# Token tiles kept in DRAM, gate stores issued by GpSimd, and MLP taps over both sequences at once, in a two-layer hybrid encoder

## The chip, the cores and the metric

The kernel runs on one core of a Trainium2 chip. Its engines are TensorE (PE, with its weight loads as PEld), VectorE (DVE), ScalarE (ACT), GpSimd (POOL) and SyncE (SP), whose instructions here only start transfers. The metric is the device time of one execution in microseconds, as the median of several runs; lower is better.

## The reference

Two sequences (a prompt of 512 tokens, a sample of 256) go through two layers of an encoder with shared weights, width 1024. What each layer computes, cut to what matters here:

```python
proj = rmsnorm(x, norm_mix) @ w_in            # z, xbc, dt, ret q/k/v/g, na q/k/v, gates
xbc  = silu(dwconv(xbc))                      # xs (512), B and C (2 x 128 each)
o_ssd = rmsnorm((bidir_scan(C, B, xs*dt_f, dt_f*a0, xs*dt_b, dt_b*a1) + d*xs) * silu(z))
o_ret = rmsnorm(bidir_scan(rotary(q), rotary(k), v)) * silu(g)      # retention
o_na  = neighborhood_attention(q, k, v, rpb)                         # on a grid 64 wide
gates = sigmoid(gates + gate_bias)
merged = sum(gates[:, :, i] * (o_i @ w_branch[i]) for i in range(3))
x = x + merged @ w_out
u = dwconv(rmsnorm(x) @ ffn_w_up)             # 3 taps a channel, zero beyond each sequence's ends
val, gt = split(u)                            # 2816 channels each
x = x + (silu(gt) * val) @ ffn_w_down
```

The scans are computed in chunks of 128 tokens: inside a chunk by a decayed score matrix, between chunks by states that run forwards and backwards.

## The kernel before

Both sequences lie side by side, T = 768 tokens in NT = 6 chunks of 128: chunks 0 to 3 are the prompt, 4 and 5 the sample. Every large product is made of three products of a high and a low part: a weight block arrives as wraw (L197, two buffers), ACT makes its high part whi (L206) and DVE the low part wlo (L207), six slots each; the products stand at L366 to L368, L388 to L390 (token-major jobs) and L492 to L494 (pairs of products).

The main stream of PE is this sequence of products: the input projection, then the gate products in pairs, then the branch products, the output projection and the MLP. The three mixers are generators (`ssd()`, `ret()`, `na()`), and `load_o()` is a fourth; a class `Side` takes a piece of one of them between main products. So their small products share PE with the main stream. The final order of each engine is set by a scheduler that simulates a timeline over the whole program; each engine then runs its instructions strictly in that order, waiting where an operand isn't there. All DMAs are issued by SP, in one row of 948 instructions, and each waits there for its operands and buffers.

The places that the change touches:

- **SSD tokens.** xbc lies in DRAM with channels in rows. `load(c)` (L762) brings a chunk as xt. `tokens(xt)` (L767) turns four blocks of it into xs (128 tokens x 512) and two into btok (128 x 256): six transposes on PE (L330, tiles xsT and bT) and two copies by ACT (L772, L777). `back(cs)` (L798) does that for chunks 3, 2, 1 and later for 5, to run the states backwards: `state()` weights xs by DVE (xw, L782) and multiplies on PE (st, L785). The chunk loop (L806) then does it again for all six chunks, since xs and btok have two buffers each. It makes the scores sc (L817), loads four decay rows a chunk, spread over partitions (cw, L827), which ACT shifts in four operations (L833) and DVE subtracts (L834), multiplies into po (L846), and on POOL starts y (L851).
- **Gates.** `gates()` (L1184): when the pair of products pg and pv is done, ACT takes its tanh (L1186) and SP stores each half to gate_scr (L1187, 384 KB each). Twelve pairs a layer; the last two take buffers of the pool that the branch loop uses. The branch loop (L1222) loads gate tiles back (g, L1233), multiplies on PE (L366 to L368) and gates the result on DVE (merged, L1238).
- **MLP.** `conv(s)` in `up()` (L1281) takes the three taps of a channel block: ACT the centre (L1285), DVE the two outer ones (L1287, L1289), once for the prompt's 512 columns and once for the sample's 256, then SiLU or the product. There are 88 of these in all.

Of the kernel before, what the change touches and what calls it, by code (L numbers as in the profile page):

```python
# [6 lines left out]
F32 = mybir.dt.float32  # L7
F32R = mybir.dt.float32r
I32 = mybir.dt.int32
AF = mybir.ActivationFunctionType  # L10
OP = mybir.AluOpType

P = 128
# [3 lines left out]
TP = 512  # L17
# [266 lines left out]
def body(tc, nc, a, depth=DEPTH):  # L284
# [303 lines left out]
    def layer(l, x_in, prev_x):  # L588
# [32 lines left out]
        nkl_scr = dram.tile([4, P, T], F32, name=f"nkl_scr{l}")  # L621
        gate_scr = dram.tile([24, P, T], F32, name=f"gate_scr{l}")
        cum_scr = dram.tile([4 * NT, 512], F32, name=f"cum_scr{l}")
        t1_scr = dram.tile([3, P, 512], F32, name=f"t1_scr{l}")
        o_scr = [dram.tile([T, 512], F32, name=f"o_scr{l}_{b}") for b in range(3)]

# [84 lines left out]
        def ssd():  # L711
# [55 lines left out]
            def tokens(xt):  # L767
# [9 lines left out]
                act(b, ps[:, :256], AF.Copy)  # L777
                return xs, b

            def state(xs, b, d, c, prev, tag, bufs):  # L780
                xw = nt([P, 8, 64], "xw", "rx", 1)
                tt(xw, xs.rearrange("p (h c) -> p h c", c=64), bc(ex[:, d, c, :, None], [P, 8, 64]), op=OP.mult)  # L782
                ps = mxbank("st", "mx")
                for g in range(2):
                    mm(ps[:, g * 256:(g + 1) * 256], b[:, g * P:(g + 1) * P],  # L785
                       xw[:, g * 4:g * 4 + 4, :], start=True, stop=True)
                new = nt([P, 512], "new", tag, bufs)
                if prev is None:
                    act(new, ps, AF.Copy)
                else:  # L790
                    tt(new.rearrange("p (h c) -> p h c", c=64), prev.rearrange("p (h c) -> p h c", c=64),
                       bc(ex[:, 4 + d, c, :, None], [P, 8, 64]), op=OP.mult)
                    tt(new, new, ps, op=OP.add)
                return new
# [3 lines left out]
            def back(cs):  # L798
                for c in cs:
                    xt = load(c)  # L800
                    xs, b = tokens(xt)
                    yield
                    pb[c - 1] = state(xs, b, 1, c, pb[c], "pb", 5)
                    yield

            for c in range(NT):  # L806
# [3 lines left out]
                xt = load(c)  # L810
                zt = nt([P, 512], "zt", "ld2", 1)
                nc.sync.dma_start(zt, z_scr[c * P:(c + 1) * P])
                xs, b = tokens(xt)
                x3 = xs.rearrange("p (h c) -> p h c", c=64)
                sc = mxbank("sc", "my")
                for g in range(2):
# [367 lines left out]
        def gates(i, pool, tag, bufs, pump):  # L1184
            def evac(j, g):
                act(g, g, AF.Tanh, bias=gbh[:, i + j:i + j + 1], scale=0.5)  # L1186
                nc.sync.dma_start(gate_scr[i + j], g)  # L1187

            pair(pool, tag, bufs, pump, evac)

# [84 lines left out]
        def up(i):  # L1275
# [5 lines left out]
            def conv(s):  # L1281
                r, u = raw[s], ftile("u", ("uv", "ug")[s])
                f = i + NFF * s
                w = lambda j: par[:, O_FW + f * 3 + j:O_FW + f * 3 + j + 1]
                act(u, r, AF.Identity, scale=w(1), bias=par[:, O_FB + f:O_FB + f + 1])  # L1285
                for c0, n in RANGES:
                    stt(u[:, c0 + 1:c0 + n], r[:, c0:c0 + n - 1], w(0), u[:, c0 + 1:c0 + n],  # L1287
                        op0=OP.mult, op1=OP.add)
                    stt(u[:, c0:c0 + n - 1], r[:, c0 + 1:c0 + n], w(2), u[:, c0:c0 + n - 1],  # L1289
                        op0=OP.mult, op1=OP.add)  # L1290
                us[s] = u
                if s == 1:
                    act(u, u, AF.Silu)
                    return
                ah, al = out
                tt(u, u, us[1], op=OP.mult)
                act(ah, u, AF.Copy)
                tt(al, u, ah.bitcast(F32), op=OP.subtract)
# [101 lines left out]
```

## Time and profile before

| | |
|---|---|
| median of 3 runs | 2604.86 us (2600.97 to 2606.41) |
| the profiled execution | 2605.65 us, its span 2603.9 us |
| mean granted clock of TensorE | 0.995 |
| busy: PE, DVE, ACT, POOL | 2560.1, 1904.2, 1153.4, 87.8 us |
| DMA | 359.65 MB, mean 138 GB/s |
| SSD in the trace | about 126 to 300 us in layer 0, 1416 to 1590 us in layer 1 |
| branch products begin | at about 622 us and 1915 us |
| MLP | up to 1290 us and up to 2584 us |

The span is the profiled execution from its first to its last instruction; the device time has a little around it. A row of a view names the line, the engine, the operation and the tiles as out<-in; in brackets stands how long the engine was idle before it, and what ended that.

### The profile page before, as it was taken

Reading aid. Unit: us, or ns where it says so; the run is one execution under the profiler, and the core shown is the slowest. Engines: PE = TensorE matmul, PEld = TensorE weight load, DVE = VectorE, ACT = ScalarE, POOL = GpSimd, SP = SyncE. Lnnn points to the kernel's source line nnn. Section 1 sums busy time; section 2 is a strip of 40 time slices with the busy share of each in tenths; the row PEclk is TensorE's granted clock in tenths of the full one; section 3 lists DMA queues with packets and bytes.
Section 4 is the critical chain, followed back from the end, with each engine's and each line's share of the span. In section 5 each row is a group of like instructions: output and inputs, shape, how many; then the busy total and the mean of one; then the engine's idle time right before and its main releaser. Section 6 shows DMA issues by size and latency. Waiting matters only on the chain.

```text
span 2603.9 us, 37538 instructions
## 1 busy us (share of the span) xinstructions
PE 2560.1 (98%) x14290; PEld 2353.6 (90%) x14290; DVE 1904.2 (73%) x3204; ACT 1153.4 (44%) x1946; POOL 87.8 (3%) x130
## 2 busy tenths in 40 slices
PE   8999999999999999999999999999999999999998
PEld 8878999999889999999998789999998899999997
DVE  6758876665658887888866688765657598888887
ACT  5434465553235433333454455655432354333343
POOL 0002100000000000000000011100000000000000
PEclk9999999999999999999999999999999999999999
DMA  7356568747522222222453575787474222212222
GB/s 248 108 169 204 190 213 255 223 134 230 158 81 67 67 70 73 65 68 71 135 174 129 163 233 172 219 236 215 132 230 141 73 89 65 62 60 73 74 66 89
DMA packets 168900, 359.65 MB, mean 138 GB/s; under 512 B 16080, under 2 KB 62480, under 8 KB 168720
## 3 DMA queue, kind: packets, MB, share of 16 engines
q1 hardware_dynamic: 168720, 357.25, 43.5%
q8 instruction: 113, 1.85, 0.3%
q14 instruction: 67, 0.55, 0.1%
HBM read 276.87 MB, written 80.31 MB: 137 GB/s over the span
## 4 chain that ended last, share of the span: by engine, by line
PE 85%; DMA 7%; ACT 3%; DVE 3%; issue 1%; SPq 1%; POOL 0%; DVEq 0%; POOLq 0%; ACTq 0%
PE acc L493 12%; PE acc L492 12%; PE acc L494 12%; PE dn L1344 5%; PE dn L1342 5%; PE dn L1343 5%; PE acc L366 4%; PE acc L368 4%; PE acc L367 4%; PE acc L389 3%; PE acc L388 3%; PE acc L390 3%; PE wo L390 2%; PE wo L388 2%; PE wo L389 2%
## 5 line engine op out<-in xcount | busy, mean ns | idle before, releaser
L206 ACT ACTIVATE whi<-wraw 128x1024 fp32r<-128x1024 f32 (+2 forms) x444 | 433.8, 985 | 616.0 <-DMA wraw<-wp 153.3
L207 DVE TENSOR_TENSOR wlo<-wraw,whi 128x1024 fp32r<-128x1024 f32 (+2 forms) x444 | 500.3, 1132 | 189.2 <-ACT whi L206 186.9
L493 PE MATMUL acc<-hTl,whi 128*128 128x384 f32 x1216 | 414.3, 341 | 5.0 <-DVE hTl L435 5.0
L492 PE MATMUL acc<-hTh,whi 128*128 128x384 f32 x1216 | 414.1, 341 | 2.9 <-ACT pt L498 2.0
L494 PE MATMUL acc<-hTh,wlo 128*128 128x384 f32 x1216 | 410.0, 339 | 0.0
L492 PE MATMUL acc<-Eh,whi 128*128 128x384 f32 x912 | 309.3, 340 | 0.9 <-DVE pv L498 0.9
L494 PE MATMUL acc<-Eh,wlo 128*128 128x384 f32 x912 | 307.4, 338 | 0.0
L493 PE MATMUL acc<-El,whi 128*128 128x384 f32 x912 | 306.9, 337 | 0.0
L493 PEld LDWEIGHTS acc<-hTl,whi 128*128 128x128 f32 x1216 | 230.3, 189 | 7.5 <-DVE hTl L435 6.0
L492 PEld LDWEIGHTS acc<-hTh,whi 128*128 128x128 f32 x1216 | 229.9, 189 | 7.4 <-ACT pt L498 3.5
L494 PEld LDWEIGHTS acc<-hTh,wlo 128*128 128x128 f32 x1216 | 229.9, 189 | 0.4
L389 PE MATMUL acc<-wlo,hTh 128*128 128x512 f32 (+1 forms) x576 | 210.1, 366 | 2.6 <-DVE wlo L207 2.6
L388 PE MATMUL acc<-whi,hTh 128*128 128x512 f32 (+1 forms) x576 | 208.8, 364 | 2.9 <-ACT whi L206 2.6
L390 PE MATMUL acc<-whi,hTl 128*128 128x512 f32 (+1 forms) x576 | 209.2, 365 | 0.0
L1343 PE MATMUL dn<-wlo,ah 128*128 128x512 f32 x528 | 207.4, 393 | 0.0
L1344 PE MATMUL dn<-whi,al 128*128 128x512 f32 x528 | 201.8, 394 | 0.0
L1342 PE MATMUL dn<-whi,ah 128*128 128x512 f32 x528 | 200.4, 393 | 0.0
L1357 DVE TENSOR_TENSOR x<-x,dn 128x512 f32<-128x512 f32 x168 | 111.9, 685 | 86.0 <-PE dn L1344 86.0
L366 PE MATMUL acc<-hTh,whi 128*128 128x256 f32 (+1 forms) x512 | 174.0, 340 | 0.0
L492 PEld LDWEIGHTS acc<-Eh,whi 128*128 128x128 f32 x912 | 171.3, 188 | 2.9 <-DVE pv L498 1.9
L368 PE MATMUL acc<-hTh,wlo 128*128 128x256 f32 (+1 forms) x512 | 172.9, 338 | 0.0
L367 PE MATMUL acc<-hTl,whi 128*128 128x256 f32 (+1 forms) x512 | 172.9, 338 | 0.0
(277 smaller groups left out, 4772.3 us busy)
## 6 DMA issues: line engine op xcount, KB each, us to landing
wraw<-wp SPq DMA_DIRECT2D x284, 512.0 KB
g<-gate_scr SPq DMA_DIRECT2D x48, 384.0 KB
cw<-cum_scr SPq DMA_DIRECT2D x48, 256.0 KB
xt<-xbc_scr SPq DMA_DIRECT2D x20, 512.0 KB
bias<-nab SPq DMA_DIRECT2D x40, 256.0 KB
gate_scr<-pg SPq DMA_DIRECT2D x24, 384.0 KB
gate_scr<-pv SPq DMA_DIRECT2D x24, 384.0 KB
ot<-o_scr SPq DMA_DIRECT2D x36, 256.0 KB
```

Source lines behind the costliest of these rows:

```text
L206: self.nc.scalar.activation(hi[:, :n], r, AF.Copy)
L207: self.nc.vector.tensor_tensor(lo[:, :n], r, hi[:, :n].bitcast(F32), op=OP.subtract)
L366: mm(o, wh[:, k, :], rh, start=(k == 0), stop=False)
L388: mm(o, hT[0][:, k, ts_], wh[:, cs], start=(k == 0), stop=False)
L389: mm(o, hT[0][:, k, ts_], wl[:, cs], start=False, stop=False)
L390: mm(o, hT[1][:, k, ts_], wh[:, cs], start=False, stop=(k == NK - 1))
L492: mm(o, w[0][:, k, :], r[0][:, k, :], start=first and k == 0, stop=False, skip_group_check=True)
L493: mm(o, w[0][:, k, :], r[1][:, k, :], start=False, stop=False, skip_group_check=True)
L494: mm(o, w[1][:, k, :], r[0][:, k, :], start=False, stop=k == 3, skip_group_check=True)
L1342: mm(ps, ah[:, tsl], wh[:, cs], start=(j == 0), stop=False)
L1343: mm(ps, ah[:, tsl], wl[:, cs], start=False, stop=False)
L1344: mm(ps, al[:, tsl], wh[:, cs], start=False, stop=(j == n - 1))
```

## The change

1. `back()` stores xs and btok of its chunks to a new DRAM buffer tok_scr; the chunk loop loads them back for chunks 1, 2, 3 and 5 and makes them by transposes only for chunks 0 and 4.
2. The gate stores are issued by POOL instead of SP.
3. The outer taps of the MLP run over all 768 columns in one operation a tap. At the border between the sequences that adds a product across the border to two columns. Three small ACT operations put that right: two compute the correct values of the two columns ahead, into a tile `end`, and one copies them in behind.

```diff
--- before.py
+++ after.py
@@ -621,6 +621,7 @@
         nkl_scr = dram.tile([4, P, T], F32, name=f"nkl_scr{l}")
         gate_scr = dram.tile([24, P, T], F32, name=f"gate_scr{l}")
         cum_scr = dram.tile([4 * NT, 512], F32, name=f"cum_scr{l}")
+        tok_scr = dram.tile([NT, P, 768], F32, name=f"tok_scr{l}")
         t1_scr = dram.tile([3, P, 512], F32, name=f"t1_scr{l}")
         o_scr = [dram.tile([T, 512], F32, name=f"o_scr{l}_{b}") for b in range(3)]
 
@@ -777,6 +778,12 @@
                 act(b, ps[:, :256], AF.Copy)
                 return xs, b
 
+            def kept_tokens(c):
+                xs, b = nt([P, 512], "xs", "tok", 2), nt([P, 256], "btok", "tb", 2)
+                nc.sync.dma_start(xs, tok_scr[c, :, :512])
+                nc.sync.dma_start(b, tok_scr[c, :, 512:])
+                return xs, b
+
             def state(xs, b, d, c, prev, tag, bufs):
                 xw = nt([P, 8, 64], "xw", "rx", 1)
                 tt(xw, xs.rearrange("p (h c) -> p h c", c=64), bc(ex[:, d, c, :, None], [P, 8, 64]), op=OP.mult)
@@ -799,6 +806,8 @@
                 for c in cs:
                     xt = load(c)
                     xs, b = tokens(xt)
+                    nc.sync.dma_start(tok_scr[c, :, :512], xs)
+                    nc.sync.dma_start(tok_scr[c, :, 512:], b)
                     yield
                     pb[c - 1] = state(xs, b, 1, c, pb[c], "pb", 5)
                     yield
@@ -810,7 +819,7 @@
                 xt = load(c)
                 zt = nt([P, 512], "zt", "ld2", 1)
                 nc.sync.dma_start(zt, z_scr[c * P:(c + 1) * P])
-                xs, b = tokens(xt)
+                xs, b = tokens(xt) if c in (0, 4) else kept_tokens(c)
                 x3 = xs.rearrange("p (h c) -> p h c", c=64)
                 sc = mxbank("sc", "my")
                 for g in range(2):
@@ -1184,7 +1193,7 @@
         def gates(i, pool, tag, bufs, pump):
             def evac(j, g):
                 act(g, g, AF.Tanh, bias=gbh[:, i + j:i + j + 1], scale=0.5)
-                nc.sync.dma_start(gate_scr[i + j], g)
+                nc.gpsimd.dma_start(gate_scr[i + j], g)
 
             pair(pool, tag, bufs, pump, evac)
 
@@ -1283,11 +1292,13 @@
                 f = i + NFF * s
                 w = lambda j: par[:, O_FW + f * 3 + j:O_FW + f * 3 + j + 1]
                 act(u, r, AF.Identity, scale=w(1), bias=par[:, O_FB + f:O_FB + f + 1])
-                for c0, n in RANGES:
-                    stt(u[:, c0 + 1:c0 + n], r[:, c0:c0 + n - 1], w(0), u[:, c0 + 1:c0 + n],
-                        op0=OP.mult, op1=OP.add)
-                    stt(u[:, c0:c0 + n - 1], r[:, c0 + 1:c0 + n], w(2), u[:, c0:c0 + n - 1],
-                        op0=OP.mult, op1=OP.add)
+
+                end = small([P, 2], "nmx", 3)
+                act(end[:, 0:1], r[:, TP - 2:TP - 1], AF.Identity, scale=w(0), bias=u[:, TP - 1:TP])
+                act(end[:, 1:2], r[:, TP + 1:TP + 2], AF.Identity, scale=w(2), bias=u[:, TP:TP + 1])
+                stt(u[:, 1:], r[:, :T - 1], w(0), u[:, 1:], op0=OP.mult, op1=OP.add)
+                stt(u[:, :T - 1], r[:, 1:], w(2), u[:, :T - 1], op0=OP.mult, op1=OP.add)
+                act(u[:, TP - 1:TP + 1], end, AF.Copy)
                 us[s] = u
                 if s == 1:
                     act(u, u, AF.Silu)
```

The scheduler places everything anew. On ACT, where the SSD of layer 0 begins (whi is the high part of a weight block, cw a spread decay row, btok the chunk's token tile that st waits for), before:

```order
L206 ACTIVATE whi_1727<-wraw_1288 128x1024
L833 ACTIVATE cw_2039<-cw_2039,ncf_1367 128x128 x4
L206 ACTIVATE whi_1733<-wraw_1294 128x1024
L777 ACTIVATE btok_1443<-bT_1440 128x256
L682 ACTIVATE rraw_1716<-acc_1666 128x512
```

and now:

```order
L206 ACTIVATE whi_1734<-wraw_1289 128x1024
L206 ACTIVATE whi_1740<-wraw_1295 128x1024
L842 ACTIVATE cw_2030<-cw_2030,ncf_1368 128x128
L778 ACTIVATE btok_1446<-bT_1443 128x256
L842 ACTIVATE cw_2030<-cw_2030,ncf_1368 128x128 x3
L683 ACTIVATE rraw_1723<-acc_1673 128x512
```

The second weight block moved ahead of the four cw activations, and btok into them. On PE at the same place, before:

```order
L388 MATMUL acc_1751<-whi_1727,hTh_91 128x512
L389 MATMUL acc_1751<-wlo_1728,hTh_91 128x512
L390 MATMUL acc_1751<-whi_1727,hTl_92 128x512
L388 MATMUL acc_1751<-whi_1727,hTh_91 128x512
L785 MATMUL st_1483<-xw_1481,btok_1443 128x256 x2
```

and now:

```order
L388 MATMUL acc_1758<-whi_1734,hTh_91 128x512
L389 MATMUL acc_1758<-wlo_1735,hTh_91 128x512
L792 MATMUL st_1488<-xw_1486,btok_1446 128x256 x2
L330 MATMUL xsT_1496<-maskident_71,xt8_1494 128x128 x4
L826 MATMUL sc_1570<-xt8_1554 128x128 x2
L390 MATMUL acc_1758<-whi_1734,hTl_92 128x512
```

The state product st stands two main products earlier. On SP, over the same stretch (cum_scr holds the decay rows), before:

```order
L827 DMA cw_1798<-cum_scr0_115 128x512
L764 DMA xt8_1489<-xbc_scr0_106 128x8x128
L827 DMA cw_1800<-cum_scr0_115 128x512
L827 DMA cw_1851<-cum_scr0_115 128x512
L694 DMA qk_scr0_107<-rout_1513 128x512
L827 DMA cw_1853<-cum_scr0_115 128x512
L827 DMA cw_1986<-cum_scr0_115 128x512
L694 DMA qk_scr0_107<-rout_1585 128x512
L827 DMA cw_1988<-cum_scr0_115 128x512
L827 DMA cw_2039<-cum_scr0_115 128x512
```

and now:

```order
L765 DMA xt8_1494<-xbc_scr0_106 128x8x128
L809 DMA tok_scr0_116<-xs_1418 128x512
L810 DMA tok_scr0_116<-btok_1423 128x256
L836 DMA cw_1799<-cum_scr0_115 128x512
L836 DMA cw_1850<-cum_scr0_115 128x512
L695 DMA qk_scr0_107<-rout_1520 128x512
L836 DMA cw_1852<-cum_scr0_115 128x512
L836 DMA cw_1977<-cum_scr0_115 128x512
L695 DMA qk_scr0_107<-rout_1592 128x512
L809 DMA tok_scr0_116<-xs_1441 128x512
L836 DMA cw_1979<-cum_scr0_115 128x512
L836 DMA cw_2030<-cum_scr0_115 128x512
```

The stores of the token tiles stand between the loads of the decay rows. On SP where the branch products of layer 0 begin (ot is a mixer's output, g a gate tile), before:

```order
L197 DMA wraw_6204<-wp 128x1024
L1187 DMA gate_scr0_114<-pg_6121 128x768
L1209 DMA ot_6441<-o_scr0_1_118 128x512
L1233 DMA g_6294<-gate_scr0_114 128x768
L1233 DMA g_6333<-gate_scr0_114 128x768
L1209 DMA ot_6480<-o_scr0_1_118 128x512
L1187 DMA gate_scr0_114<-pv_6120 128x768
L197 DMA wraw_6232<-wp 128x1024
```

and now:

```order
L197 DMA wraw_6181<-wp 128x1024
L1242 DMA g_6271<-gate_scr0_114 128x768
L1242 DMA g_6310<-gate_scr0_114 128x768
L1218 DMA ot_6457<-o_scr0_1_119 128x512
L1218 DMA ot_6496<-o_scr0_1_119 128x512
L197 DMA wraw_6209<-wp 128x1024
```

The two stores are gone from SP's row; they are the last two of 24 in POOL's row of this layer.

## Rows read from the trace of the kernel before

**Rows 1.** The page: busy time of each engine, and the chain that ended last by engine.

```profile
PE 2560.1 (98%) x14290; PEld 2353.6 (90%) x14290; DVE 1904.2 (73%) x3204; ACT 1153.4 (44%) x1946; POOL 87.8 (3%) x130
...
PE 85%; DMA 7%; ACT 3%; DVE 3%; issue 1%; SPq 1%; POOL 0%; DVEq 0%; POOLq 0%; ACTq 0%
```

**Rows 2.** The table of windows: from and to in us, length, busy us of PE, PEld, DVE, ACT and POOL with the count of instructions, granted clock of PE, DMA share and GB/s. In order: start and second part of the SSD and the MLP of layer 0, start and second part of the SSD of layer 1, the start of the branch products of layer 0, the neighbourhood attention of layer 1.

```profile
126.00:172.00 46.00, 42.36 (x192) 34.16 (x191) 28.94 (x70) 19.90 (x49) 0.00 (x0) 0.96 0.62 185
172.00:300.00 128.00, 128.00 (x648) 108.28 (x647) 97.70 (x203) 56.23 (x122) 23.81 (x20) 1.00 0.57 186
803.00:1290.00 487.00, 487.00 (x2548) 454.97 (x2547) 400.66 (x598) 201.24 (x241) 0.00 (x0) 1.00 0.24 73
1416.00:1458.00 42.00, 39.06 (x178) 31.22 (x177) 25.46 (x66) 19.60 (x48) 0.00 (x0) 0.96 0.59 179
1458.00:1590.00 132.00, 132.00 (x669) 112.01 (x669) 101.44 (x208) 58.97 (x125) 21.03 (x20) 1.00 0.59 191
580.00:625.00 45.00, 42.26 (x251) 39.73 (x251) 25.53 (x36) 21.27 (x29) 0.00 (x0) 1.00 0.69 222
1700.00:1780.00 80.00, 75.06 (x477) 73.79 (x476) 46.47 (x117) 39.48 (x87) 0.61 (x1) 0.96 0.84 237
```

**Rows 3.** The timeline of PE at one visit of the chunk loop (start, us, what), and by tile the transposes into xsT and ACT's copies of it (ns: shortest, median, longest).

```profile
216.53 0.40 PE L389 MATMUL acc<-wlo,hTh 128*128 128x512 f32 x1
216.76 0.60 PE L330 MATMUL xsT<-maskident,xt 128*128 128x128 f32 x4
...
217.65 0.39 PE L388 MATMUL acc<-whi,hTh 128*128 128x512 f32 x1
...
218.34 0.39 PE L390 MATMUL acc<-whi,hTl 128*128 128x512 f32 x1
218.57 0.39 PE L388 MATMUL acc<-whi,hTh 128*128 128x512 f32 x1
...
L330 PE MATMUL xsT<-maskident,xt x80: 270/272/421, 141.8 to 1558.3; 128*128 128x128 f32 x80
L772 ACT ACTIVATE xs<-xsT x20: 577/583/600, 146.1 to 1560.2; 128x512 f32<-128x512 f32 x20
```

**Rows 4.** The timeline of all engines at the start of the SSD of layer 0.

```profile
164.70 1.28 ACT L833 ACTIVATE cw<-cw,ncf 128x128 f32<-128x128 f32 x4 [2.06 <-DMA cw<-cum_scr]
...
165.89 1.04 ACT L206 ACTIVATE whi<-wraw 128x1024 fp32r<-128x1024 f32 x1
166.84 0.36 ACT L777 ACTIVATE btok<-bT 128x256 f32<-128x256 f32 x1
...
167.25 1.83 PE L785 MATMUL st<-xw,btok 128*128 128x256 f32 x4 [1.94 <-ACT btok L777]
```

**Rows 5.** PE's waits in 1416 to 1460 us, the start of the SSD of layer 1: us in total, times, longest.

```profile
PE st L785 <- ACT btok L777: 1.6, 1, 1.6
```

**Rows 6.** The table of windows, the stretch behind that wait in layer 0 and in layer 1; the third number from the end is the granted clock.

```profile
167.60:170.90 3.30, 3.30 (x13) 2.91 (x12) 3.23 (x8) 1.14 (x2) 0.00 (x0) 0.50 0.71 232
1454.40:1457.70 3.30, 3.00 (x10) 2.54 (x11) 3.22 (x7) 1.79 (x3) 0.00 (x0) 0.50 0.75 230
```

**Rows 7.** The chain that ended last between 136 and 170 us: of its four pieces on loads of the decay rows the shortest and the longest (start, us, what).

```profile
144.35 3.38 DMA cw<-cum_scr
...
160.33 4.35 DMA cw<-cum_scr
```

**Rows 8.** What SP's row waited for over the whole span (us in total, times, longest), the two rows of the gate stores.

```profile
SPq L1187 <- ACT pv L1186: 52.3, 15, 5.8
SPq L1187 <- ACT pg L1186: 43.2, 14, 4.2
```

**Rows 9.** The start of the branch products: the tanh in the timeline of layer 0, pieces of the chain behind it in layer 0 and in layer 1, and PE's wait in layer 0.

```profile
611.09 0.94 ACT L1186 ACTIVATE pg<-pg,gbh 128x768 f32<-128x768 f32 x1
...
612.60 4.90 DMA gate_scr<-pg
617.52 3.42 DMA g<-gate_scr
...
1906.56 4.64 DMA gate_scr<-pg
...
PE acc L366 <- DVE merged L1238: 1.3, 1, 1.3
```

**Rows 10.** POOL's operation on y, by tile (ns: shortest, median, longest).

```profile
L851 POOL TENSOR_TENSOR y<-xs,par x12: 1043/1968/6180, 182.4 to 1565.4; 128x512 f32<-128x512 f32 x12
```

**Rows 11.** ACT's wait behind the store of the pair before the last, in the timeline.

```profile
597.61 0.49 ACT L498 ACTIVATE pt<-acc 128x384 f32<-128x384 f32 x1 [2.71 <-DMA gate_scr<-pg]
```

**Rows 12.** The groups by form in the MLP of layer 0 (count, busy us, mean ns, idle before): an outer tap over the prompt and one over the sample; and ACT's smallest operation in the timeline.

```profile
L1287 DVE SCALAR_TENSOR_TENSOR u<-rv,par,u 128x511 f32<-128x511 f32 x22 | 16.5, 748 | 3.5 <-ACT u L1285 3.5
...
L1289 DVE SCALAR_TENSOR_TENSOR u<-rg,par,u 128x255 f32<-128x255 f32 x22 | 10.6, 480 | 0.0
...
298.62 0.20 ACT L957 ACTIVATE tk<-tk 128x8 f32<-128x8 f32 x1
```

**Rows 13.** The window of the retention of layer 1, and PE's largest waits there and in the neighbourhood attention behind it.

```profile
1590.00:1700.00 110.00, 108.32 (x700) 106.44 (x699) 84.97 (x126) 67.52 (x154) 8.13 (x12) 1.00 0.67 206
...
PE qT L330 <- ACT qd L1005: 0.9, 1, 0.9
...
PE nsc L1101 <- DMA q<-nq_scr: 2.3, 1, 2.3
```

## The prediction

> **What bounds the kernel now.** I read the page's busy line first: TensorE (PE) is busy for 2560.1 of 2603.9 us, and the chain that ended last is PE for 85% [rows 1]. VectorE (DVE, 1904.2 us) and ScalarE (ACT, 1153.4 us) can save much without moving the end; only PE's own work and PE's waits count. The table of windows then says where PE waits [rows 2]. In the MLP it never does (487.00 of 487 us in layer 0), nor in the second part of the SSD (128.00 of 128, 132.00 of 132), where main products and side work share PE. It waits about 3.6 and 2.9 us where the SSD begins, 2.7 us where the branch products of layer 0 begin, and 4.9 us at the neighbourhood attention of layer 1. So an instruction taken off PE is worth its time in the second part of the SSD, a wait removed is worth its length in three short places, and ACT or DVE time saved in the MLP is worth nothing.
>
> **Transposes taken out of the chunk loop.** Eight visits (chunks 1, 2, 3 and 5 of two layers) lose six transposes and two ACT copies each. The PE timeline of one visit prices it: from the L389 product at 216.53 to the L388 product at 217.65 are 1.12 us for two steps of the main stream, which otherwise go at 0.23 (218.34 to 218.57), so six transposes push the stream back by 1.12 - 0.46 = 0.66 us [rows 3]. PE is full there, so 8 x 0.66 = **5.3 us** leave the path. The ACT copies (583 ns for the larger, [rows 3]) go too; ACT is busy 56 of 128 us in that stretch [rows 2], so that gives nothing. In their place SP issues two loads a visit (256 and 128 KB). The DMA share there is 0.57 to 0.59, and the loads stand well ahead of their use in SP's row, so I cost them at nothing; if that cover fails, po waits for xs (rival D).
>
> **The start of the SSD.** Here the order shown above matters more than the stores themselves. Before, ACT takes one weight split (whi), then the four cw activations, which wait 2.06 us for a DMA, then the next whi (1.04), and only then btok; PE's st waits 1.94 us for btok and starts at 167.25 [rows 4]. Now the second whi stands ahead of the cw wait and fills it, and btok comes after the first of the four cw: 164.70 + 0.32 + 0.36, so st can start at about 165.45, and it stands two main products (0.46) earlier in PE's row. The gain is 167.25 - 165.45 - 0.46 = 1.34 us. Layer 1's wait for the same tile is 1.6 instead of 1.9 us [rows 5]; scaled by that, 1.13. Together **2.4 us**. Right after each of these waits PE goes at 0.50 of its clock (the 1.2 GHz level) for 3.3 us [rows 6], some 1.7 us lost each time. Whether the shorter wait keeps the clock up I can't read, so I take 0 and keep 3.4 for the range. Against it: the token stores stand on SP between the cw loads, and these loads already are the chain here, 3.4 to 4.4 us each [rows 7]. Two stores (256 and 128 KB) ahead of the second cw pair and one of 256 KB before the last pair cost two or three issues of about 0.33 us on SP, and their bytes. If that makes the last cw land 1.2 us later, the gain is gone (rival B).
>
> **Gate stores from GpSimd.** 48 stores move from SP to GpSimd (POOL). SP waited 43.2 and 52.3 us for the tanh of these tiles, and whatever stood behind waited with it [rows 8]; but PE waits for nothing that SP loads behind those places, so I take 0. Who waits for the stores is another matter. At the branch start the chain runs: tanh of pg at 611.09 to 612.03, store issued 612.60, landing 617.50, then the g load of 3.42 us, merged, and PE; in layer 1 the store takes 4.64 [rows 9]. PE waits 1.3 us at the end of it, so each microsecond more in the store is one on PE. POOL has nothing else to do there, so the issue no longer stands behind SP's wraw: 612.60 - 612.03 = 0.57 earlier. In the trace of before no DMA comes from POOL, so its lateness has no row. The nearest is POOL's only long operation, y, one shape with spans of 1.04 to 6.18 us [rows 10]: a bound of 0 to 5.1 us. I take 1.0, nearer to the lower end, because the median there (1.97) is 0.9 over the shortest and no pair but the last two is urgent: net 0.4 a layer, **+0.8 us**. The same store, one pair earlier, makes ACT's pt wait 2.71 us [rows 11], without a wait of PE behind it.
>
> The Trainium skill speaks against this edit. Its page SBUF — State Buffer (section "SBUF: two separate sides", the note on DVE blocking DMA) says that descriptors of a DMA issued from GpSimd are written by GpSimd's own cores, which certain DVE operations lock out, so that a transfer of 620 ns took 3100; by that, an estimate, each urgent store would be 2.5 us later instead of 1.0, and the sum 3 us higher. The spread of y fits such a lock, but no run here shows a store under it. It is part of rival C below.
>
> What queues behind POOL's stores: in its row the store of a pair can stand ahead of the retention's rstd (L418, L419), which then waits for a tanh. PE's waits in the retention are under 1 us each [rows 13], and I take 0.
>
> **MLP taps.** Per convolution DVE does four operations now, 748 and 480 ns twice (2.46 us); two over 767 columns take, by the slope of these rows, about 1.02 each. ACT gets three operations of two columns or fewer, about 0.2 each by its smallest rows [rows 12]: 0.6. PE has no wait in 487 us, so the term is **0** either way: DVE's saving of 88 x 0.4 = 37 us gives nothing, and ACT's 88 x 0.6 = 53 us costs nothing as long as 201 of 487 us are busy and a convolution has the next products' time to finish in. If that cover is gone it is rival E.
>
> **Moves that nobody asked for.** Retention work shifts by 2 to 35 main products against the main stream. In layer 1 PE idles 1.7 us in the retention and, as said, 4.9 in the attention; the waits there hang on ACT and on a load of q [rows 13]. I take 0, with 4 us either way.
>
> **Sum.** -5.3 - 2.4 + 0.8 = -6.9. The profiled execution took 2605.65 us (span 2603.9), 0.8 above the median of the runs, so 2598.8 on its scale and 2598 on that of the median.
>
> **Rivals.**
> B, the start of the SSD gives nothing: the stores delay the cw loads. 2604.86 - 5.3 + 0.8 = 2600.4. For it: the cw loads are the chain; against: DMA share is 0.62 there, not full.
> C, slower: POOL's gate stores land late. Place: the last pair at the branch start and, one pair earlier, pt. With the upper bound of 5.1 less the 0.57 earlier issue, 4.5 a layer; a wait of that length brings a stretch at half clock, 1.7 by [rows 6]; half of another 5.1 at pt. That is 2 x 8.7 = 17.5 against gains of 7.7: 2614.7 (2608 to 2620). It makes the kernel slower by more than 0.2% once the lateness costs PE over 6.5 us a layer. For it: PE already waits at the end of this chain; against: DVE has gaps in this stretch (25.5 of 45 us busy).
> D, the PE time freed in the chunk loop is lost again, since a kept token tile is loaded only when its buffer is free and then po waits, say 1 us in 8 visits: 2606. Against: in the order the loads stand a whole chunk ahead.
> E, slower: ACT's small operations reach PE in the MLP. One convolution in two on the path gives 44 x 0.6 = 26 us: 2624 at a sum that is otherwise mine. Against: no wait of PE there at all.
> That the change doesn't do what it says: the order shows 48 transposes fewer and 48 stores on POOL, so no chance.
>
> **How the numbers follow.** Forecast 2598, own range 2590 (clock kept, shifts helpful) to 2601; chance 0.58. B 0.19, C 0.11, D 0.07, E 0.05. A measurement can tell 0.2%, that is 5.2 us: faster is below 2599.6, slower above 2610.1. Of the forecast's 0.58 some 0.05 lie above 2599.6. So faster 0.53; same 0.05 + 0.19 + 0.07 + 0.02 of C = 0.33; slower 0.09 + 0.05 = 0.14. The range leaves out E and the upper half of C: 2589 to 2611.
>
> **What would show it.** Step one: PE busy about 13 us less in its rows (48 transposes of 272 ns, which overlap) and no xsT rows in visits 1, 2, 3, 5; the SSD windows 2.6 us shorter in each layer. Step two: PE's wait of st for btok under 0.7 us; if it is still 1.5 and the cw landings are over 5 us, it is B. Step three: PE's first L366 waits for merged 1 to 2 us; if 4 or more, it is C. Step four: no wait of PE in the MLP. The forecast is wrong if PE shows new waits in the chunk loop on xs or btok, or if the retention's shift opens gaps of several microseconds.

## The result

| | before | changed |
|---|---|---|
| median of 4 runs | 2603.09 us (2600.97 to 2606.41) | 2635.65 us (2629.43 to 2640.59) |
| ratio | | 1.0119, 95% interval 1.0097 to 1.0142 |
| span of the profiled execution | 2603.9 us | 2638.8 us |

The change makes the kernel 1.2% slower, about 32 us. Seven us faster was forecast (2598), and the range ended at 2611. The profiled execution of the changed kernel, from which all its stage times below come, is the slowest of its four. One disturbed execution of run e8 below (9252.8 us) is left out of its median.

The page of the changed kernel, against [rows 1]: span, busy time, and the queue of the stores that GpSimd issues.

```profile
span 2638.8 us, 37667 instructions
...
PE 2567.0 (97%) x14242; PEld 2355.6 (89%) x14242; DVE 1892.0 (72%) x3028; ACT 1212.2 (46%) x2194; POOL 104.0 (4%) x178
...
q0 software_dynamic: 3840, 18.88, 1.8%
```

PE has 48 instructions fewer and DVE is 12 us less busy, as the change intends, and the span is 35 us longer: PE's busy time grew by 7 (part of it runs at half clock) and its idle time by 28. So the question is where PE waits. PE's waits over the whole span of the changed kernel (us in total, times, longest):

```profile
PE nsc L1110 <- DMA q<-nq_scr: 9.3, 2, 5.2
PE tp L330 <- DVE xn L427: 8.8, 2, 7.9
PE acc L492 <- DVE rg L498: 8.3, 2, 4.2
PE acc L493 <- DVE hTl L435: 5.0, 4, 1.8
PE acc L492 <- ACT pt L498: 4.6, 6, 1.3
PE st L792 <- ACT btok L778: 3.8, 4, 1.6
PE oT L330 <- DMA ot<-o_scr: 3.6, 4, 1.1
...
PE acc L366 <- DVE merged L1247: 3.0, 2, 1.5
```

An eviction is an operation of ACT or DVE that takes a finished product out of its accumulator, so that PE can use it again. Most of the growth is in four of these rows: the attention's first products (nsc) wait for q, 9.3 us instead of one wait of 2.3 [rows 13]; PE waits for an eviction (rg) in the MLP, where it had no wait in 487 us [rows 2]; the waits for the branches' inputs (oT) are new; merged takes 3.0 over both layers instead of 1.6 (1.3 of it in layer 0 [rows 9]). The wait for the eviction pt grew too, from 2.0 to 4.6 in pieces of at most 1.3.

To see what each stage gains or loses I paired the nth main product (tiles acc, dn, wo: 12,192 in each trace) of a run with the nth of the kernel before and took the difference of their starts; its growth over a stage is what that stage lost. Each entry comes from one execution. At 395 us the kernel before has a gap of 2.8 us in its main stream, which PE fills with side work, so the split between retention and attention is good to about 2 us only; their sum is firmer. All stages by this method, in us, for the runs told below too (stage ends in the time of the kernel before: SSD 126 to 300, retention to 395, attention to 500, branch start 580 to 660, MLP start 800 to 905; in layer 1 1416 to 1590, 1690, 1800, 1885 to 1960, 2080 to 2145):

| run | SSD | ret. | att. | branch | MLP | SSD | ret. | att. | branch | MLP |
|---|---|---|---|---|---|---|---|---|---|---|
| changed kernel | +0.2 | -2.9 | +10.7 | +2.9 | +6.8 | -0.7 | +4.0 | +2.0 | +2.7 | +7.8 |
| e1 tokens | -3.5 | -2.1 | +7.8 | +2.1 | 0.0 | +0.5 | -0.4 | +0.3 | +1.4 | +0.2 |
| e2 gates | +0.8 | +1.3 | -0.5 | +5.1 | -0.1 | +1.3 | +0.2 | -6.1 | +3.3 | +0.1 |
| e3 taps | -1.1 | +1.8 | -0.5 | -1.0 | +8.0 | -0.4 | -0.1 | -6.6 | +0.9 | +6.5 |
| e13 taps, own tile | +1.0 | +0.5 | -0.2 | +0.4 | +1.0 | +0.6 | -0.3 | -6.7 | +1.1 | +1.1 |

The profiled execution of the kernel before lost some 6 us in the attention of layer 1 that its other executions needn't have: the seven runs below that make the tokens as before (e2, e3, e7, e10 to e13) stand at -5.8 to -7.0 there. The changed kernel's +2.0 is therefore a loss of about 8.

So the SSD gives little, the attention takes about 19 us over both layers, the branch start 6, and the MLP 15, nearly all of it at its first pair of products (the rest of the MLP loses 1.0 and 0.6). The same places can be seen on the timeline. The attention of layer 0, pieces of the chain of the changed kernel (start, us, what):

```profile
419.83 0.61 SPq L1090
...
423.86 8.58 DMA nv<-nv_scr
...
433.64 7.81 DMA q<-nq_scr
...
441.50 0.58 PE nsc L1110
```

SP starts the attention's loads at 419.8, 3.7 us later than before (416.1), while PE's main stream is 2.8 us ahead of its old time at 395. The products meet loads that aren't there.

### The profile page after: what moved, and what is told of

It is laid out like the page before. It is cut to its first block, busy times and chain, and to the rows that moved or that the text cites. A ratio compares the mean times of both kernels' runs of the same rounds, so it can differ in the third digit from the quotient of the medians.

```text
span 2638.8 us, 37667 instructions
## 1 busy us (share of the span) xinstructions
PE 2567.0 (97%) x14242; PEld 2355.6 (89%) x14242; DVE 1892.0 (72%) x3028; ACT 1212.2 (46%) x2194; POOL 104.0 (4%) x178
## 4 chain that ended last, share of the span: by engine, by line
PE 62%; issue 8%; DMA 7%; DVE 5%; ACT 2%; POOL 0%; SPq 0%; DVEq 0%; POOLq 0%; ACTq 0%
PE acc L492 9%; PE acc L493 9%; PE acc L494 9%; PE dn L1355 5%; PE dn L1353 5%; PE dn L1354 5%; PE acc L366 3%; PE acc L367 3%; PE acc L368 3%; DMA wraw<-wp 3%; PE wo L390 2%; PE wo L388 2%; PE wo L389 2%; DMA cw<-cum_scr 1%; PE acc L388 1%
## 5 line engine op out<-in xcount | busy, mean ns | idle before, releaser
L217 DVE TENSOR_TENSOR wraw<-wraw 128x512 f32<-128x512 f32 x228 | 157.3, 690 | 33.9 <-DMA wraw<-wp 30.9
L493 PEld LDWEIGHTS acc<-El,whi 128*128 128x128 f32 x912 | 173.0, 190 | 0.5
```

What stands on the lines that cost most here:

```text
L493: mm(o, w[0][:, k, :], r[1][:, k, :], start=False, stop=False, skip_group_check=True)
```

## The experiments

Ratios are against the kernel before on the same chip, with their 95% interval.

### One part at a time

The three parts of the diff above, each alone, and the first two together.

> Only the token tiles are kept in DRAM; gate stores stay on SP and the taps stay as they were. Theory (by stages of the changed kernel's trace): the order of the SSD, of the retention and of the attention's first rows is the changed kernel's, so this run shows its loss at the attention: the SSD gives 0 net, the attention loses 7.9 us in layer 0 and about 5 in layer 1; about 2616. Rival (the gate stores cause the attention's loss, because the rstd of the retention queues behind them on GpSimd): the attention loses nothing here and the run shows the transposes' gain, about 2598.

Measured: 1.0019 (1.0008 to 1.0030), 2608.88 us.

> Only the gate stores move to GpSimd. Theory: the start of the branch products loses about 3 us a layer because of what the scheduler moves there, the attention is near that of before; about 2609. Rival (the gate stores cause the attention's loss): 8 and 5 us are lost at the attention as well, about 2622.

Measured: 1.0033 (1.0021 to 1.0045), 2612.87 us.

> Only the MLP's outer taps run over both sequences, with the three small ACT operations. Theory: PE stalls once per layer, at the first pair of products of the MLP, 4.2 us with a stretch at half clock behind it, 7.5 us a layer in all; then nothing: about 2618. Rival (the small ACT operations delay PE all through the MLP): a loss spread over all 44 pairs, 20 us or more, about 2624 or above.

Measured: 1.0054 (1.0038 to 1.0070), 2618.43 us.

> Tokens in DRAM and gate stores on GpSimd, the taps as before: the change without its third part. Theory (the losses stand in different stages and add): the changed kernel less 15 us, about 2620. Rival (the parts interact, since the order of the branch start is another one when both are there): more than 5 us away from the sum of the two parts alone.

Measured: 1.0051 (1.0037 to 1.0065), 2618.86 us. The parts alone add to 0.52% for the first two and 1.06% for all three; the change has 1.19% (0.97 to 1.42). Within the intervals they add, and no part is a gain. The table shows each in its stage: the tokens' loss at the attention, the gates' at the branch start, the taps' at the start of the MLP. My expectation for the tokens (2616) was 7 us too high; it was read from the changed kernel's profiled execution, which is 5 us above the median of its four.

### The taps: not the operations, a shared buffer name

> Only the merged taps, without the three small ACT operations: the two columns at the border between the sequences keep the product across the border. In the order the first convolution's taps stand where they stood before. Theory (the small ACT operations push the first convolution behind the next weight blocks and in front of an eviction that PE waits for): no stall at the start of the MLP, 2603 within 2 us. Rival (the wider DVE operations hold the evictions up): the stall is there, 2618.

Against e3:

```diff
-                end = small([P, 2], "nmx", 3)
-                act(end[:, 0:1], ...)
-                act(end[:, 1:2], ...)
                 stt(u[:, 1:], ...)
                 stt(u[:, :T - 1], ...)
-                act(u[:, TP - 1:TP + 1], end, AF.Copy)
```

Measured: 1.0020 (1.0011 to 1.0028), 2606.78 us: by the ratios about 9 us better than e3, though not level with before and outside the 2603 within 2 of the expectation. The trace shows no stall at the start of the MLP (by the paired products the main stream stands at -0.6 us at 800 and at 905). What is left stands later in the MLP, 2 us in layer 0 and 3 in layer 1, with waits of at most 1.0 us for evictions.

> The taps in four operations as before, with the three small ACT operations added (they write what already stands there). Theory (the small ACT operations move the first convolution's taps): the stall at the start of the MLP is there, as in the taps run, 2618. Rival (the wide DVE operations are needed for it): 2604.

Against the kernel before:

```diff
+                end = small([P, 2], "nmx", 3)
+                act(end[:, 0:1], ...)
+                act(end[:, 1:2], ...)
                 for c0, n in RANGES:
                     ...
+                act(u[:, TP - 1:TP + 1], end, AF.Copy)
```

Measured: 1.0069 (1.0057 to 1.0081), 2622.06 us. The stall is there without any wide operation, here at the eviction of the other half. PE's wait at 815 to 860 us of this run:

```profile
PE acc L492 <- ACT rv L498: 5.4, 1, 5.4
```

> The change's taps with their small ACT operations in every pair of the MLP but the first of each layer, which has the taps as before. Theory (the loss stands at the first pair alone; in the rest PE waits for neither engine): 2603 within 2 us. Rival (ACT's small operations cost PE a little in every pair): 2608 or more.

Against the kernel before:

```diff
+                if i == 0:
+                    for c0, n in RANGES:
+                        ...
+                else:
+                    end = small([P, 2], "nmx", 3)
+                    ...
```

Measured: 0.9997 (0.9986 to 1.0007), 2602.95 us. So 42 of 44 pairs neither gain nor lose by the change.

What is special in the first pair stands in the order of DVE. There the value half (rv) is ready before the gate half (rg), and before the change its taps ran at once. Before:

```order
L498 SCALAR_TENSOR_TENSOR rv_7751<-acc_7818,pt_7755 128x384
L207 TENSOR_TENSOR wlo_7906<-wraw_7422,whi_7905 128x1024
L1287 SCALAR_TENSOR_TENSOR u_7929<-rv_7751,par_98,u_7929 128x511
```

In e3 the first of them comes 14 rows behind that eviction of rv instead of 2, behind the first tap of the gate half and ahead of the eviction that PE waits for:

```order
L1290 SCALAR_TENSOR_TENSOR u_7922<-rg_7752,par_98,u_7922 128x767
L1290 SCALAR_TENSOR_TENSOR u_7931<-rv_7751,par_98,u_7931 128x767
L1291 SCALAR_TENSOR_TENSOR u_7922<-rg_7752,par_98,u_7922 128x767
L207 TENSOR_TENSOR wlo_8007<-wraw_7430,whi_8006 128x1024
L1291 SCALAR_TENSOR_TENSOR u_7931<-rv_7751,par_98,u_7931 128x767
L498 TENSOR_TENSOR rg_7943<-acc_7961,pt_7946 128x384
```

The same on the timeline of the changed kernel, DVE and ACT at the start of the MLP of layer 0 (start, us, what, idle before):

```profile
831.86 0.39 ACT L1297 ACTIVATE nmx<-rg,u,par 128x1 f32<-128x1 f32 x1
...
832.43 0.37 ACT L1297 ACTIVATE nmx<-rv,u,par 128x1 f32<-128x1 f32 x1
...
833.82 1.01 DVE L1299 SCALAR_TENSOR_TENSOR u<-rv,par,u 128x767 f32<-128x767 f32 x1
834.75 1.01 DVE L1300 SCALAR_TENSOR_TENSOR u<-rg,par,u 128x767 f32<-128x767 f32 x1
835.68 1.22 DVE L207 TENSOR_TENSOR wlo<-wraw,whi 128x1024 fp32r<-128x1024 f32 x1
...
836.81 1.01 DVE L1300 SCALAR_TENSOR_TENSOR u<-rv,par,u 128x767 f32<-128x767 f32 x1
...
837.74 0.55 DVE L498 TENSOR_TENSOR rg<-acc,pt 128x384 f32<-128x384 f32 x1
...
838.43 0.66 PE L492 MATMUL acc<-hTh,whi 128*128 128x384 f32 x1 [4.18 <-DVE rg L498]
```

The border values (nmx) of rv come right behind those of rg. Both halves take that tile from one rotating name, and the program asks for rg's first. e13 gives each half its own name, and alters nothing else of e3:

```diff
-                end = small([P, 2], "nmx", 3)
+                end = small([P, 2], *(("ssq2", 4) if s else ("nmx", 3)))
```

> Only the change's taps, with all three small ACT operations in every pair, but the two halves take their tile of border values from two buffer names. In the order the first convolution's taps stand where they stood before. Theory (sharing one name ties the value half's convolution behind the gate half's, and that is the whole stall): no stall, 2603 within 2 us. Rival (the small ACT operations cost it by their time): 2618.

Measured: 1.0006 (0.9996 to 1.0015), 2603.21 us. PE's wait at 815 to 860 us in this run, where e3 and the changed kernel have 4.2:

```profile
PE acc L492 <- ACT rv L498: 0.7, 1, 0.7
```

> The whole change with that one name altered. Theory: the changed kernel less the 15 us of the MLP's starts, 2619 within 3 us. Rival: 2633.

Measured: 1.0064 (1.0049 to 1.0078), 2619.45 us: this one name is worth 0.55% of the change's 1.19%. The cause of the taps' part is settled.

The stall of 4.2 us costs about 7 a layer, because PE comes out of it at half clock: the wait and half of the 4.77 us that PE is busy in the window below make 6.6. The window begins inside the wait, 2 us before its end (changed kernel, columns as in [rows 6]):

```profile
836.40:843.20 6.80, 4.77 (x15) 4.80 (x16) 6.18 (x10) 5.15 (x9) 0.00 (x0) 0.50 0.27 81
```

### The gates: the last two pairs

> Only the last two of the twelve gate pairs are stored by GpSimd. In the order the transposes of the branches' inputs (oT) stand where they do when all go by GpSimd, and the attention stands as before. Theory (the branch start loses because oT moved ahead of what its loads deliver): nearly all of the gate run's loss, about 2611. Rival (the loss comes from the twenty other stores on GpSimd, or from the landing of the last store): 2604 or less in the first case; in the second the landing of the last pair's store would be over 6.5 us.

Against the kernel before:

```diff
-                nc.sync.dma_start(gate_scr[i + j], g)
+                (nc.sync if i < NG1 else nc.gpsimd).dma_start(gate_scr[i + j], g)
```

Measured: 1.0038 (1.0025 to 1.0050), 2611.40 us. Of its trace only the order is read.

> The first ten of the twelve gate pairs are stored by GpSimd, the last two by SP as before. Theory (the gate run's loss stands at the branch start and comes with the last two pairs): 2604 within 2 us. Rival (stores on GpSimd as such, or the shift of the attention's first rows by 3 to 9 main products, cost time): 2608 or more.

The same edit with the engines exchanged. Measured: 1.0006 (0.9996 to 1.0015), 2606.01 us. So the loss comes with the last two pairs. The landing of the stores is the smaller part of it: at the branch start of the changed kernel the timeline of ACT and of POOL has

```profile
621.31 0.93 ACT L1195 ACTIVATE pg<-pg,gbh 128x768 f32<-128x768 f32 x1
...
622.65 0.54 POOL L1196 DMA_DIRECT2D gate_scr<-pg  x1 [10.67 <-ACT pg L1195]
```

and the chain that ended last, behind them,

```profile
628.28 3.12 DMA g<-gate_scr
```

from the tanh's end (622.24) to the g load 6.0 us, against 5.5 before (612.03 to 617.52 [rows 9]); in layer 1 5.25 against 5.06. What is late in the changed kernel is PE itself: by the paired products the 2.9 us of layer 0 are lost by 610 us, and 2.0 of layer 1's by 1912, ahead of the wait for merged. PE's waits at 575 to 660 us in e2, which had none for ot before:

```profile
PE acc L366 <- DVE merged L1238: 2.9, 1, 2.9
PE oT L330 <- DMA ot<-o_scr: 1.5, 2, 1.0
```

With the stores out of SP's row the scheduler moves transposes of the branches' inputs (oT), in e2 from 36 main products earlier to 24 later, and PE reaches some before their load has landed. In e2 2 us of layer 0 are lost there and 2.6 in layer 1. The other 3 us of its layer 0 stand at the wait for merged, 2.9 us instead of 1.3, behind which PE goes at half clock for 3.4 us. The tanh and the g load in front of that wait, in e2:

```profile
612.70 0.92 ACT L1186 ACTIVATE pg<-pg,gbh 128x768 f32<-128x768 f32 x1
...
619.55 4.34 DMA g<-gate_scr
```

That is 5.9 us to the load instead of 5.5, and a load of 4.34 us instead of 3.42; why this load took longer isn't shown, and the changed kernel's (3.12) didn't. That e8 has the same moves of oT in both layers and the same loss fits the account by oT; so does e12, whose layer 1 moves oT in part with the last stores still on SP and loses 0.9 us ahead of merged. But no run kept oT's old place with all stores on GpSimd, so the moves of oT as the cause are argued, not shown.

### The tokens: the loss stands at the attention

> Tokens kept for chunks 1, 2 and 3 only; chunk 5 is transposed a second time, as before. In the order the retention's last products stand 10 main products later than before instead of 17 to 24, since chunk 5 no longer goes through a store and a load at the end of the SSD. Theory (the attention's loads stand on SP right behind the retention's last store, so a late retention makes PE wait there): the loss at the attention shrinks to half or less, and with 6 x 0.66 us of transposes gone the run gives about 2602. Rival (the bytes and SP issues of the copies cost the time, not the retention's place): the loss stays that of the token run alone, about 2608.

Against e1:

```diff
-                    nc.sync.dma_start(tok_scr[c, :, :512], xs)
-                    nc.sync.dma_start(tok_scr[c, :, 512:], b)
+                    if c < 4:
+                        nc.sync.dma_start(tok_scr[c, :, :512], xs)
+                        nc.sync.dma_start(tok_scr[c, :, 512:], b)
...
-                xs, b = tokens(xt) if c in (0, 4) else kept_tokens(c)
+                xs, b = tokens(xt) if c in (0, 4, 5) else kept_tokens(c)
```

Measured: 1.0008 (0.9999 to 1.0017), 2604.77 us. The wait of nsc for q is 3.6 us in total instead of 10.0 in e1, and the attention of layer 0 loses 4.9 instead of 7.8 (retention and attention together 5.2 instead of 5.7). What e5 gains over e1 stands for the most part in the attention of layer 1, -4.9 instead of +0.3. PE's wait in e1, over the whole span:

```profile
PE nsc L1110 <- DMA q<-nq_scr: 10.0, 4, 4.4
```

> As the run before it in this call, with the token stores issued by GpSimd. In the order the retention now stands 2 to 34 main products earlier than in the kernel before. Theory: PE doesn't wait for the attention's loads at all, the transposes' 4 us come through: about 2599. Rival (the copies themselves cost it): 2606 or more.

As e5, with `nc.gpsimd` for the stores to tok_scr. Measured: 1.0007 (0.9998 to 1.0016), 2604.61 us. PE's waits for q are no longer in the list of its waits, and there is no loss in the attention (-0.1 in layer 0), but no gain either: the SSD and the retention lose 2.0 us in layer 0 by the paired products (from -1.7 at 126 to +0.3 at 395), with PE waiting 3.3 us for xt and 2.2 for an eviction of pg there. In layer 1 its attention stands at -2.5, against -5.8 to -7.0 in the runs with the tokens as before, so it isn't free of the loss.

> Nothing is kept in DRAM: the chunk loop transposes only btok for chunks 1, 2, 3 and 5 and uses the xs of chunk 0 or 4 in their place, so four transposes and one ACT copy a visit are left out and the mixer's result is another one. No store or load is added. In a visit whose transposes stand apart, the four of xsT push the main stream back by 0.43 us, so 8 x 0.43 = 3.4 us are at stake. Theory (PE time freed in the SSD comes through unless the copies or a late retention take it back): about 2599.5. Rival (the stages behind take back whatever is freed ahead of them): 2603.

Against the kernel before:

```diff
-            def tokens(xt):
+            def tokens(xt, xs=None):
...
-                xs, b = tokens(xt)
+                xs, b = tokens(xt, None if c in (0, 4) else xs)
```

Measured: 1.0037 (1.0024 to 1.0051), 2614.83 us. With an xs given, tokens makes only btok: 32 transposes less, no transfer more, and 10 us slower. Both statements of the expectation fall. The order moves here as in e6, and PE's waits in 172 to 300 us and in 300 to 395 us of this run are

```profile
PE sc L818 <- DMA xt<-xbc_scr: 3.1, 1, 3.1
...
PE acc L492 <- DVE pg L498: 2.1, 1, 2.1
```

> The token run with the retention's output stores on GpSimd; the retention ends as late in the order as in the token run, the attention's first products stand 22 main products later than before instead of 11. Theory (PE comes to the attention's first products too early for their loads): the wait for q shrinks from 10 us in total to under 5, about 2603. Rival (the copies themselves cost the time): 2608 as the token run.

The token run with `nc.gpsimd` for the retention's output stores. Measured: 1.0021 (1.0011 to 1.0032), 2608.02 us. The wait for q fell to 1.0 us as the theory said, and the loss stayed: the attention of layer 0 takes 10.5 us, now as waits in 395 to 510 us for other things:

```profile
PE acc L492 <- DVE pv L498: 2.5, 1, 2.5
PE npo L1133 <- DMA nv<-nv_scr: 1.9, 2, 1.2
PE rpo L1035 <- DVE rm L1031: 1.0, 1, 1.0
PE nsc L1110 <- DMA q<-nq_scr: 1.0, 1, 1.0
```

So q was the place where the wait showed, not its cause.

What holds in layer 0 over four token runs, e1, e5, e15 and the changed kernel, is this. SP starts the attention's loads at 415.8 us in e1, 416.8 in e5, 418.8 in e15, 419.8 in the changed kernel (416.1 before), while at 395 us the main stream is 7.2, 3.7, 4.3 and 2.8 us ahead. At 500 us it stands at +0.6, +1.2, +6.2 and +7.9. The first of these loads on SP before and in e1:

```profile
416.10 0.39 SPq L1081 DMA_DIRECT2D kh<-nk_scr  x1
...
415.76 0.38 SPq L1090 DMA_DIRECT2D kh<-nk_scr  x1
```

So the main products are ahead, the loads start no earlier by as much, and at the attention PE waits. That the PE time saved makes this lead isn't shown. Part of the lead is the order: 1740 main products stand ahead of the retention's last product in e1, e15 and the changed kernel, 1733 in e5 and 1723 before, and 17 of them take about 3 us at 0.17 us each. And e9, which saves PE time too but has the retention earlier in the order (1704), is some 5 us behind at 395 us, not ahead.

In layer 1 the attention stands at +2.0 in the changed kernel and at -1.3 to +0.4 in e1, e4, e14 and e15, at -4.9 in e5 and -1.6 in e9, against -5.8 to -7.0 in the seven runs with the tokens as before. The loss is there as well, also where nothing is copied.

> The three parts in their mended forms: tokens kept for chunks 1, 2 and 3, the first ten gate pairs on GpSimd, the taps with two buffer names. Theory (each part alone is within noise of before and they stand in different stages): 2604 within 3 us, not slower than before by more than 0.2%. Rival (the attention's first products, now up to 28 main products later, open a new wait): 2610 or more.

Measured: 1.0035 (1.0023 to 1.0048), 2611.39 us. Three parts that are each level with before make 9 us together, spread over several stages (attention of layer 0 +4.1, MLP start +1.9, retention of layer 1 +1.5). The time is that of the rival. Whether a new wait makes it (nv, 1.5 us in the attention of layer 0) isn't shown: the three ratios alone add to 0.20%, and what is left to 0.35% is within the intervals. Nothing here beats the kernel before.

## Why the prediction was wrong

**The step that failed** is "Moves that nobody asked for": I had seen that the scheduler moves retention work by up to 35 main products, took 0, and gave it 4 us either way; the branches' inputs weren't in it. The runs put about 19 us there at the attention over both layers and some 5 at the branch start. The second is "MLP taps, 0", whose condition failed at the first pair of each layer: 15 us. All three losses stand where the order moved. I had priced what the change adds and removes on each engine, and the price was in where the rest went. The prediction's own last sign, gaps of several microseconds behind the retention's shift, is what came.

**Transposes, -5.3.** This term holds where it was read. In the second part of the SSD the five runs that keep all tokens (the changed kernel, e1, e4, e14, e15) are on average 1.0 us shorter than the kernel before in layer 0 and 1.9 in layer 1, the seven with the tokens as before 1.2 and 1.0 longer: together some 5 us. Rival D isn't it either: no product waits for a token tile loaded from tok_scr. But the attention took more than that back: e1's retention and attention of layer 0 lose 5.7 us. That PE time taken from the side work only lets the main stream arrive earlier at its next wait for side work is my reading; e9 speaks against it as a rule.

**Start of the SSD, -2.4.** Wrong: by the paired products the same five runs stand 0.6 us below the seven others there in layer 0 and 1.3 above them in layer 1. PE's waits for btok in the timeline of the changed kernel, against [rows 4]:

```profile
166.29 0.40 ACT L842 ACTIVATE cw<-cw,ncf 128x128 f32<-128x128 f32 x1 [1.28 <-DMA cw<-cum_scr]
166.60 0.36 ACT L778 ACTIVATE btok<-bT 128x256 f32<-128x256 f32 x1
...
167.02 1.74 PE L792 MATMUL st<-xw,btok 128*128 128x256 f32 x4 [1.14 <-ACT btok L778]
```

The wait is 1.1 instead of 1.9 us in layer 0 and the same 1.6 in layer 1: the cw load, which I had taken at 164.70, let ACT go on only at 166.29, 1.6 us later. The outcome is that of rival B, which named 1.2. Its mechanism isn't shown. Its sign was a load of over 5 us, and from issue to ACT it took 4.6 us, before 4.8; SP issued the pair later. The issue before and in the changed kernel:

```profile
159.91 1.01 SPq L827 DMA_DIRECT2D cw<-cum_scr  x2
...
161.74 0.79 SPq L836 DMA_DIRECT2D cw<-cum_scr  x2
```

The clock still fell behind the wait.

**Gate stores, +0.8.** The sum for the last store was near: from tanh to g load 0.5 us later in layer 0 and 0.2 in layer 1 (0.4 and 0.6 in e2), against 0.4 a layer. That is partly luck, since two sizes were too large and cancel: from issue to g load it takes 0.2 to 0.7 us longer than from SP, not 1.0, and the issue stands 0.2 us or less earlier behind the tanh, not 0.57. Rival C, with 4.5 us a layer, is refuted. The Trainium skill's page SBUF — State Buffer (SBUF: two separate sides) has the 2.5 us for a DMA beside a DVE copy; here the stores ran beside other DVE operations, tensor_tensor and scalar_tensor_tensor for the most part, and no such delay shows. The 48 stores land in 2.6 to 7.3 us, 4.1 in the median, and GpSimd is occupied 0.54 us by most. The loss of about 3 us a layer is for the most part another one, through oT, which I didn't have.

**MLP taps, 0.** Right for 42 of 44 pairs, and e13 shows it for all: ACT's added time is free. (DVE's saving was mis-sized: its taps' busy time fell by 26 us, not 37, since the durations that I added up overlap; it gives nothing either way.) Rival E named ACT's small operations, with a loss spread over the pairs; they did cost 15 us, by a constraint on the order in two places. "As long as a convolution has the next products' time to finish in" didn't hold where DVE's row put the eviction behind it.

**What stays open:** which move makes the attention wait in the token runs, why e6, whose attention starts its loads at 411.5 us, gains nothing by it, and which waits cause which in e9 and e16. The runs show that the losses go with the order; they don't hold the order still while one duration changes, so the share of each wait isn't settled.

## What to carry to other kernels

Where a scheduler orders every engine, compare the whole order before and after and put a price on each move that makes a product meet its load or its eviction earlier; such moves cost 30 to 40 us here, and the work taken off PE was worth 5. A new small tile that two pieces of work take from one rotating buffer name ties them to program order: give each its own name, and look in the order whether anything else moved. Time taken off a full engine didn't count here, since the waits in the stages behind grew by more: before summing, follow the side chains that the engine waits for next, in the new order, to their end.

## What the runs showed of the hardware

In the changed kernel the granted clock of TensorE fell to 0.50 inside a PE wait of 4.2 us in the MLP and stayed there for 6.8 us. The length of such a stretch didn't follow that of the wait: behind the wait of 1.6 us for btok in layer 1 it was 3.3 us before [rows 6] and 6.8 in the changed kernel, and behind the wait of 4.2 us in the MLP of layer 1 of e3 it was 3.4. The last two windows:

```profile
1471.30:1478.10 6.80, 5.40 (x17) 4.55 (x18) 5.07 (x10) 3.53 (x8) 0.00 (x0) 0.50 0.98 302
...
2122.20:2125.60 3.40, 3.40 (x12) 3.40 (x11) 2.87 (x5) 2.15 (x5) 0.00 (x0) 0.50 0.11 43
```

A store of 384 KB issued by GpSimd held that engine for 0.54 us and landed in 4.1 us in the median; from its issue to the load behind it at the branch start it took 0.2 to 0.7 us longer than one issued by SP (4.85 against 4.66 us in layer 1 of the changed kernel, 5.63 against 4.92 in layer 0).
